# The state space gates as one product of 512 columns with the tokens at rest, in place of two of 256

## The chip, the core and the metric

The kernel runs on one core of a Trainium2 chip. Its time is device microseconds from the start to the end of one execution. Three runs of the kernel before gave a median of 1881.25 us (1880.52 to 1882.83). In the text PE is TensorE, DVE is VectorE, ACT is ScalarE, POOL is GpSimd and SP is the engine whose queue issues nearly all the DMAs.

## What is computed

A backbone of two layers over 256 latent and 256 context tokens of width 1024. Each layer is a half-step SwiGLU, a token mixer and a second half-step SwiGLU. The mixer projects the normalized tokens with `w_in`, splits the columns over three parallel groups (a gated linear recurrence of width 256, an attention of width 256, and a state space scan of width 512), and joins their outputs with `w_out`. In the last layer only the latent tokens go on behind the mixer. The change touches the columns z of `w_in`, 512 of them, which gate the state space part:

```
def mamba2_output(y, xs, z, d_skip, w):
    b, L = y.shape[:2]
    y = (y + d_skip[:, None] * xs).reshape(b, L, D_SSM)
    return rms_norm(y * jax.nn.silu(z), w)
...
    out_lat = jnp.concatenate([hg_lat, na_lat, ssm_lat], axis=-1) @ w_out
```

## The kernel before

All 512 tokens (context in columns 0 to 255, latent behind) stay on the core, features on the partitions, as eight tiles of 128 features. Every float32 product is made of three matmuls on rounded halves: a weight chunk `raw` of 128 x 1024 is loaded by SP, ACT casts it to `hi` (L291), DVE subtracts to get `lo` (L294), and `mm3` (L675 to L677) runs high by high, high by low and low by high. A chunk holds eight blocks of 128 columns in the order of `weight_plan`; `hi` and `lo` have two buffers each, `raw` three.

PSUM has eight banks, handed out by tags d, e, m and n with two each. A tile of a tag waits until the tile that held its buffer has been read. Tag n serves the attention's scores and transposes (`psm("n")`), tag d the projections.

Most projections keep a weight block at rest and stream 512 tokens. Some keep tokens at rest: 128 tokens of `hh` and `hl` are the stationary operand, and weight columns are streamed. The gates z are such a product. `tokens` makes 256 columns for each token tile and puts two token tiles into one bank, so that four token tiles take two banks of tag d (layer 0) and two take one (layer 1, where only the latent tiles 2 and 3 are needed). This is done twice, for the two halves of z; each half is evicted by ACT with Silu into `zs` (tag gm, L1400). Behind the state space scan `ssm` multiplies by `zs` (L1382), takes the mean square (L1383), normalizes, transposes (L1391) and splits into `mx` for `w_out`.

The order of the mixer is a list written by hand, `MIX_ORDER`: "feat", "feats", "feats1" and "tok" are dense projections, "go" starts a generator (`hg` for the recurrence, `na` for the attention, `ssm` for the scan) and "run" lets the started generators go on. The gates come last, behind all generators. The framework's scheduler then reorders the instructions of each engine within what the data and the buffers allow, so that dense matmuls come to stand between the steps of the generators. In a generator's step of attention, PE makes the scores of one head and one token tile (L1191) into a tile of tag n, DVE adds the bias (L1194, latent tiles only) and takes the maximum (L1196), ACT takes the exponential (L1198), PE transposes (L1203) into the other tile of tag n, ACT copies it (L1205), and PE multiplies by the values (L1207) into the scores' tile. Context tiles have 256 keys, latent tiles 512. After the last head the outputs are normalized (L1215, Newton steps from L557, L1218), transposed into two more tiles of tag n (L1223) and read by ACT and DVE (L873, L874). The recurrence `hg` has six levels of PE scores (L1069), DVE products (L1094) and an ACT copy (L1083), then transposes (L1105), state updates (L1116, L1127) and outputs (L1139, L1141, L1149, L1159). The scan has state updates (L1313, L1317, L1330), and for each token tile a product L1342, masks L1346, and weights L1366 to L1369 for the matmul L1374. `w_out` begins with the halves of the recurrence and the attention; its banks have the tags d, d, m, m, n, n in layer 0 and d, d, m, m in layer 1.

Of the kernel before, what the change touches and what calls it, by code (L numbers as in the profile page):

```python
# [12 lines left out]
AF = mybir.ActivationFunctionType  # L13
# [4 lines left out]
P = 128  # L18
KT = D // P
# [27 lines left out]
C_QA, C_KA, C_VA = 1280, 1536, 1792  # L47
C_Z, C_XBC, C_DT = 2048, 2560, 3584
# [44 lines left out]
def weight_plan(layer):  # L93

    plan, twice = [], []

    def align():
        plan.extend([None] * (-len(plan) % CB))

    def use_twice(blocks):  # L100
        align()
        n = len(plan) // CB
        plan.extend(blocks)
        align()
        twice.extend(range(n, len(plan) // CB))

    def ffn(w13, w2, passes, lat_only):
        for fs in FPARTS:
            rest = list(fs)
            if fs is FPARTS[0]:  # L110
                group, rest = rest[:2], rest[2:]
                blocks = [(w13, k, c, P) for k in range(KT) for f in group for c in (f * P, DFF + f * P)]
                plan.extend(blocks + blocks[:-2 * CB] * (passes - 1))
            for f in rest:
                for c in (f * P, DFF + f * P):
                    plan.extend((w13, k, c, P) for k in range(KT))
            tail = [] if lat_only or fs is not FPARTS[-1] else TAIL_F
            for d in range(KT):
                if d not in tail:
                    plan.extend((w2, f, d * P, P) for f in fs)  # L120
            if tail:
                use_twice([(w2, f, d * P, P) for d in tail for f in fs])
        align()

    def feat(c):
        plan.extend(("w_in", k, c, P) for k in range(KT))

    def tok(c):
        if c == C_VA:

            for k in range(0, KT, 3):
                align()
                plan.extend(("w_in", j, a, n) for j in range(k, min(k + 3, KT)) for a, n in ((c, 256), (C_DT, 16)))
                align()
            return
        for k in range(KT):
            plan.extend(("w_in", k, c + j, P) for j in (0, P))

    last = layer == DEPTH - 1
    ffn("ffn1_w13", "ffn1_w2", 1 if layer == 0 else 2, False)  # L140
    for step in MIX_ORDER[layer]:
        if step[0] in ("feats", "feats1"):
            blocks = [("w_in", k, c, P) for k in range(KT) for c in step[1:]]
            plan.extend(blocks + (blocks[:-2 * CB] if step[0] == "feats" else []))
        elif step[0] == "feat":
            feat(step[1])
        elif step[0] == "tok":
            tok(step[1])
    for ks in WOUT_K[layer]:
        for d in range(WOUT_N[layer]):  # L150
            plan.extend(("w_out", k, d * P, P) for k in ks)
    if not last:
        use_twice([("w_out", k, d * P, P) for d in TAIL_D for k in range(KT)])
    ffn("ffn2_w13", "ffn2_w2", 1 if last else 2, last)
    return plan, twice


def second(n):
# [17 lines left out]
        ("feat", C_C), ("run", 2), ("run", 4), ("feat", C_XS), ("feat", C_XS + 128), ("feat", C_XS + 256),  # L176
        ("feat", C_KA), ("dt",), ("go", "ssm"), ("run", 999), ("feat", C_QA), ("feat", C_KA + 128),
        ("go", "na"), ("run", 999), ("feats1", C_FF + 128, C_FB + 128, C_Q + 128, C_G + 128), ("go", "hg", 1),
        ("run", 999), ("tok", C_Z), ("tok", C_Z + 256), ("run", 999),
    ],  # L180
    [
        ("feats", C_FF, C_FB, C_Q, C_G), ("go", "hg", 0), ("tok", C_I), ("run", 999), ("tok", C_VA),
# [1 line left out]
        ("feat", C_B + 128), ("feat", C_C), ("feats1", C_FF + 128, C_FB + 128, C_Q + 128, C_G + 128),  # L184
        ("go", "hg", 1), ("run", 999), ("feat", C_XS), ("feat", C_XS + 128), ("feat", C_XS + 256),
        ("feat", C_XS + 384), ("dt",), ("go", "ssm"), ("run", 999), ("feat", C_KA + 128),
        ("feat", C_QA + 128), ("go", "na"), ("run", 999), ("tok", C_Z), ("tok", C_Z + 256), ("run", 999),
    ],
]

# [1 line left out]
def host_layout(inp):  # L192
# [39 lines left out]
    for l in range(DEPTH):  # L232
        plan = weight_plan(l)[0]
        for i in range(0, len(plan), CB):
            w, o = np.zeros((P, CB * P), np.float32), 0
            for name, k, c, n in filter(None, plan[i:i + CB]):
                w[:, o:o + n] = g[name][l][k * P:(k + 1) * P, c:c + n]
                o += n
            chunks.append(w)
# [15 lines left out]
class Weights:  # L255


    def __init__(self, b):
        self.b = b
        self.n = 0  # L260
        self.loads, self.raws = 0, []
        self.splits, self.parts = 0, []
        self.hold = 0
        self.at = 0
        self.after = ()
        self.twice = set()
        n = 0
        for l in range(DEPTH):
            plan, twice = weight_plan(l)
            self.twice.update(n + c for c in twice)  # L270
            n += len(plan) // CB
        self.chunks = n
# [73 lines left out]
class Build:  # L346
# [576 lines left out]
    def mixer(self, l, last):  # L923
        tc = self.tc
        self.l, self.last = l, last
        self.lo = CTX if last else 0
        self.tts = [2, 3] if last else [0, 1, 2, 3]
        self.mx = {}
        self.have = set()
        self.gs, self.qk, self.xf, self.bc = {}, {}, {}, {}  # L930
        self.active = {}
        with tc.tile_pool(name=self.nm("px"), bufs=1, reuse_waits="tile") as self.px:

            self.nc.sync.dma_start(out=self.xd, in_=self.x)
            self.xt4, self.ys4 = self.x[:, 0:4], self.x[:, 4:8]
            lat_only = (C_Q, C_G, C_QA, C_C)
            for step in MIX_ORDER[l]:
                if step[0] in ("feat", "feats", "feats1"):
                    cs = step[1:]
                    lo = [self.lo if any(b <= c < b + 256 for b in lat_only) else 0 for c in cs]  # L940
                    if len(cs) == 1:
                        pss = [self.feat([(lo[0], T)])]
                    elif step[0] == "feats1":
                        pss = self.group([(0, T)], "ddmm", lo)
                    else:
                        pss = self.group([(0, CTX), (CTX, T)], los=lo)
                    for c, lo, ps in zip(cs, lo, pss):
                        self.feature(c, lo, ps)
                elif step[0] == "tok":
                    c = step[1]  # L950
                    if c == C_VA:
                        self.va_in(self.tokens_dt())
                    else:
                        ps = self.tokens(self.tts if c >= C_Z else [0, 1, 2, 3])
                        if c >= C_Z:
                            self.z_in((c - C_Z) // 256, ps)
                        else:
                            self.v_in(ps)
                    self.have.add(c)
                elif step[0] == "go":  # L960
                    self.active[getattr(self, step[1])(*step[2:])] = None
                elif step[0] == "run":
                    self.pump(step[1])
                else:
                    getattr(self, step[0])()
            self.pump()
            assert not self.active
            if self.stop == "mix_%d" % l:
                self.dump_mix()
                return  # L970
            for k in range(0, KT, 2):
                self.nc.sync.dma_start(out=self.x[:, k:k + 2], in_=self.xd[:, k:k + 2])
            self.w_out(l, last)
            if last:
                self.raw_rstd()
                self.head = self.raw_group()
# [318 lines left out]
    def ssm(self):  # L1295
# [13 lines left out]
        for i in range(3):  # L1309
            for d in range(2):  # L1310
                t, t2 = order[d][i], order[d][i + 1]
# [3 lines left out]
                ps = self.psm("e")  # L1315
# [21 lines left out]
        for t in self.tts:  # L1337
            s = slice(t * P, (t + 1) * P)
# [9 lines left out]
            for g in range(2):  # L1348
                pa = self.psm("e")
                for d, m in ((0, self.slr), (1, self.sur)):  # L1350
                    for i, src in enumerate((self.ah, self.al)):
                        gm = self.tt("gm", [P, 4, P], F32R)
# [22 lines left out]
                                     start=True, stop=True)  # L1375
                nc.vector.tensor_tensor(out=y[:, gs], in0=y[:, gs], in1=py[:, :256], op=ALU.add)
                yield
        yield lambda: C_Z in self.have and C_Z + 256 in self.have
        nt = len(self.tts)
        ss = self.small([P, 4], "sss", 1)  # L1380
        for i, t in enumerate(self.tts):
# [11 lines left out]
            self.mx[4 + f] = self.split(mk, lo, T, pf[:, lo:], self.p(l, "ssn", f))  # L1393
            yield

    def z_in(self, j, ps):
        if j == 0:
            self.zs = {t: self.tt("gm", [P, 512]) for t in self.tts}
        for t in self.tts:
            self.nc.scalar.activation(self.zs[t][:, j * 256:j * 256 + 256], ps[t], AF.Silu)  # L1400

    def w_out(self, l, last):
        nc = self.nc
# [158 lines left out]
```

## Time and profile before

| | before |
|---|---|
| median of 3 runs | 1881.25 us (1880.52 to 1882.83) |
| the profiled execution, its own time | 1881.97 us |
| its span, first to last instruction | 1880.2 us |
| PE busy in the span | 1852.1 us, 99% |
| DVE busy | 1317.0 us, 70% |
| ACT busy | 724.8 us, 39% |
| POOL busy | 59.3 us, 3% |
| mean granted clock of PE, as a share of full speed | 0.995 |

The busy time of an engine is the time in which at least one of its instructions was running. The granted clock is the share of PE's full clock that the chip let through. All times of rows below are microseconds from the start of the span of this one execution, the durations of single instructions in the grouped list nanoseconds.

### The profile page before, as it was taken

Reading aid. Unit: us, or ns where it says so; the run is one execution under the profiler, and the core shown is the slowest. Engines: PE = TensorE matmul, PEld = TensorE weight load, DVE = VectorE, ACT = ScalarE, POOL = GpSimd, SP = SyncE. Lnnn points to the kernel's source line nnn. Section 1 sums busy time; section 2 is a strip of 40 time slices with the busy share of each in tenths; the row PEclk is TensorE's granted clock in tenths of the full one; section 3 lists DMA queues with packets and bytes.
Section 4 is the critical chain, followed back from the end, with each engine's and each line's share of the span. In section 5 each row is a group of like instructions: output and inputs, shape, how many; then the busy total and the mean of one; then the engine's idle time right before and its main releaser. Section 6 shows DMA issues by size and latency. Waiting matters only on the chain.

```text
span 1880.2 us, 28238 instructions
## 1 busy us (share of the span) xinstructions
PE 1852.1 (99%) x11235; PEld 1596.1 (85%) x11235; DVE 1317.0 (70%) x2324; ACT 724.8 (39%) x1160; POOL 59.3 (3%) x76
## 2 busy tenths in 40 slices
PE   9999999999999999999999999999999999999998
PEld 7788888899777889888888898888889987889998
DVE  7677877875877677677733557777637668887565
ACT  4332223334425544232223342222234455465454
POOL 1000000000014000000000000000000000210000
PEclk9999999999999999999999999999999999999999
DMA  8466666634212134566533536666434422245554
GB/s 307 156 193 194 197 190 194 185 138 124 79 40 62 47 116 143 163 195 192 163 94 101 158 112 189 193 194 194 126 101 154 144 91 74 91 142 183 181 180 134
DMA packets 76964, 277.83 MB, mean 148 GB/s; under 512 B 8608, under 2 KB 10016, under 8 KB 76320
## 3 DMA queue, kind: packets, MB, share of 16 engines
q1 hardware_dynamic: 75312, 272.88, 46.2%
q10 hardware_dynamic: 1520, 3.15, 0.5%
q8 instruction: 88, 1.44, 0.3%
q14 instruction: 44, 0.36, 0.1%
HBM read 269.71 MB, written 5.24 MB: 146 GB/s over the span
## 4 chain that ended last, share of the span: by engine, by line
PE 92%; DVE 6%; ACT 1%; issue 1%; DMA 0%; SPq 0%; DVEq 0%; ACTq 0%
PE psd L675 28%; PE psd L676 27%; PE psd L677 27%; PE psm L1069 1%; DVE junk L516 1%; PE psm L1191 1%; PE psm L1207 1%; PE psm L1317 1%; PE psm L1374 1%; DVE ew L1367 1%; PE psm L1330 1%; DVE lo L294 0%; PE psm L1358 0%; PE psm L592 0%; PE psm L578 0%
## 5 line engine op out<-in xcount | busy, mean ns | idle before, releaser
L294 DVE TENSOR_TENSOR lo<-raw,hi 128x1024 fp32r<-128x1024 f32 x328 | 403.7, 1231 | 369.0 <-ACT hi L291 365.4
L291 ACT CAST hi<-raw 128x1024 fp32r<-128x1024 f32 x332 | 348.6, 1050 | 715.8 <-PE psd L676 664.5
L675 PE MATMUL psd<-h,hi 128*128 128x512 f32 (+1 forms) x1456 | 539.0, 372 | 2.0 <-ACT h L655 1.0
L676 PE MATMUL psd<-h,hi 128*128 128x512 f32 (+1 forms) x1456 | 537.7, 370 | 0.5 <-DVE h L656 0.5
L677 PE MATMUL psd<-h,lo 128*128 128x512 f32 (+1 forms) x1456 | 536.5, 370 | 0.2 <-DVE lo L294 0.2
L516 DVE CUSTOM_DVE_ANT_0 junk<-wm,csb,par 128x1024 bf16<-128x1024 f32 x256 | 327.8, 1280 | 2.4
L675 PEld LDWEIGHTS psd<-h,hi 128*128 128x128 f32 x1456 | 273.5, 189 | 50.0 <-issue 1.5
L677 PEld LDWEIGHTS psd<-h,lo 128*128 128x128 f32 x1456 | 274.1, 188 | 48.4 <-issue 1.5
L676 PEld LDWEIGHTS psd<-h,hi 128*128 128x128 f32 x1456 | 274.6, 189 | 45.6 <-DVE h L656 0.9
L675 PE MATMUL psd<-gh,hi 128*128 128x512 f32 (+1 forms) x605 | 216.8, 358 | 0.0
L677 PE MATMUL psd<-gh,lo 128*128 128x512 f32 (+1 forms) x605 | 216.4, 358 | 0.0
L676 PE MATMUL psd<-gl,hi 128*128 128x512 f32 (+1 forms) x605 | 216.4, 358 | 0.0
L675 PEld LDWEIGHTS psd<-gh,hi 128*128 128x128 f32 x605 | 114.3, 189 | 17.0 <-ACT gh L813 0.3
L676 PEld LDWEIGHTS psd<-gl,hi 128*128 128x128 f32 x605 | 114.2, 189 | 16.7
L677 PEld LDWEIGHTS psd<-gh,lo 128*128 128x128 f32 x605 | 114.2, 189 | 16.7
L676 PE MATMUL psd<-raw,hi 128*128 128x258 f32 x352 | 99.7, 284 | 0.0
L675 PE MATMUL psd<-raw,hi 128*128 128x258 f32 x352 | 99.6, 284 | 0.0
L677 PE MATMUL psd<-raw,lo 128*128 128x258 f32 x352 | 99.3, 284 | 0.0
L813 ACT CAST gh<-silu 128x512 fp32r<-128x512 f32 (+1 forms) x88 | 49.7, 566 | 86.0 <-DVE silu L810 83.6
L544 DVE SCALAR_TENSOR_TENSOR x<-psd,gate,x 128x256 f32<-128x256 f32 x112 | 52.0, 480 | 36.6 <-PE psd L677 35.8
L675 PE MATMUL psd<-hi,h 128*128 128x256 f32 (+1 forms) x224 | 65.9, 295 | 1.4 <-ACT ga L1037 1.3
L675 PEld LDWEIGHTS psd<-raw,hi 128*128 128x128 f32 x352 | 67.0, 190 | 0.0
(276 smaller groups left out, 2435.5 us busy)
## 6 DMA issues: line engine op xcount, KB each, us to landing
raw<-in_wst SPq DMA_DIRECT2D x349, 512.0 KB, 3.6
wm<-in_wmod SPq DMA_DIRECT2D x128, 512.0 KB, 4.1
ws<-in_wm SPq DMA_DIRECT2D x8, 512.0 KB, 9.9
xd<-x SPq DMA_DIRECT2D x2, 2048.0 KB, 6.5
x<-xd SPq DMA_DIRECT2D x8, 512.0 KB, 4.1
wc<-in_wmod SPq DMA_DIRECT2D x7, 512.0 KB, 10.0
x<-in_xt SPq DMA_DIRECT2D x4, 512.0 KB, 5.3
n<-in_bias SPq DMA_DIRECT2D x8, 256.0 KB, 3.3
```

Source lines behind the costliest of these rows:

```text
L291: cut = nc.scalar.copy(hi, r)
L294: ins = e.tensor_tensor(out=lo, in0=r, in1=hi.bitcast(F32), op=ALU.subtract)
L516: self.nc.vector.tensor_tensor_reduce(junk, w, self.csb[:, v], 1.0, self.p(l, "bmod", j), ALU.mult, ALU.add, accum_out=self.mod[l][:, j, v ...
L544: ins = nc.vector.scalar_tensor_tensor(out=self.x[:, d, a:b], in0=ps[:, a - off:b - off], scalar=gate[:, d, v:v + 1], in1=self.x[:, d, a:b ...
L675: mm(ps, wh, xh, start=start, stop=False)
L676: mm(ps, wh, xl, start=False, stop=False)
L677: mm(ps, wl, xh, start=False, stop=stop)
L813: nc.scalar.copy(a[:, lo:hi], s[:, lo:hi])
L1069: nc.tensor.matmul(ps[r, s], kc[r, s], q(r, c * 64), start=True, stop=True)
L1191: nc.tensor.matmul(ps[:, :nk], self.qk[h2][r, t * P:(t + 1) * P], self.qk[2 + h2][r, :nk], start=True, stop=True)
L1207: nc.tensor.matmul(ps[:, hc], pT[:, k * P:(k + 1) * P], self.V[:, k, 256 + h * 64:256 + h * 64 + 64], start=k == 0, stop=k == nk // P - 1)
L1317: nc.tensor.matmul(ps[:, g * 256:g * 256 + 256], bt[:, t, g * P:(g + 1) * P], xw[:, g * 256:g * 256 + 256], start=True, stop=True)
```

## The change

The two products of 256 columns become one of 512: for each of the eight feature tiles k, four weight blocks (512 columns, half a chunk) are streamed against each token tile at rest. Each token tile has a bank of its own, of the tags d, d, n, n in layer 0 and d, d in layer 1. The matmuls are half as many and twice as wide (192 to 96 in layer 0, 96 to 48 in layer 1, the three of each `mm3` counted). The weights' order in the plan follows. Silu evicts 512 columns at a time.

```
         elif step[0] == "tok":
             tok(step[1])
+        elif step[0] == "gates":
+            plan.extend(("w_in", k, C_Z + j * P, P) for k in range(KT) for j in range(4))
...
-        ("run", 999), ("tok", C_Z), ("tok", C_Z + 256), ("run", 999),
+        ("run", 999), ("gates",), ("run", 999),
...
-        ("feat", C_QA + 128), ("go", "na"), ("run", 999), ("tok", C_Z), ("tok", C_Z + 256), ("run", 999),
+        ("feat", C_QA + 128), ("go", "na"), ("run", 999), ("gates",), ("run", 999),
...
-        yield lambda: C_Z in self.have and C_Z + 256 in self.have
+        yield lambda: C_Z in self.have
...
-    def z_in(self, j, ps):
-        if j == 0:
-            self.zs = {t: self.tt("gm", [P, 512]) for t in self.tts}
-        for t in self.tts:
-            self.nc.scalar.activation(self.zs[t][:, j * 256:j * 256 + 256], ps[t], AF.Silu)
+    def gates(self):
+
+        banks = [self.psd(tag) for tag in "ddnn"[:len(self.tts)]]
+        for k in range(KT):
+            wh, wl = self.w.next(4)
+            for t, q in zip(self.tts, banks):
+                s = slice(t * P, (t + 1) * P)
+                self.mm3(q, self.hh[k][:, s], self.hl[k][:, s], wh, wl, k == 0, k == KT - 1)
+        self.zs = {t: self.tt("gm", [P, 512]) for t in self.tts}
+        for t, q in zip(self.tts, banks):
+            self.nc.scalar.activation(self.zs[t], q, AF.Silu)
+        self.have.add(C_Z)
```

The scheduler decides where these matmuls stand on PE. In the rows below lines are those of the kernel that the rows come from; in the changed kernel the mixer's lines up to here are 2 lower (L1201 there is L1203 before) and those of `mm3` 2 higher (L677 is L675). `psm` are the small products' tiles of PSUM, `psd` those of the projections, `h` the normalized tokens, `con` holds the identity, `n` the attention's probabilities, `V` the values, `qk` queries and keys, `ga` the recurrence's factors.

Place 1 is PE in layer 0, in the attention's rounds over latent tokens. The kernel before has between the transposes of one head (L1203) and the values of that head (L1207) gate matmuls, into banks psd_5874 and psd_5875:

```order
L1203 MATMUL psm_5240<-con,n_897_5237 128x128 x4
L675 MATMUL psd_5874<-hi_5814,h_3213 128x256
L676 MATMUL psd_5874<-lo_5815,h_3213 128x256
L677 MATMUL psd_5874<-hi_5814,h_3214 128x256
L675 MATMUL psd_5874<-hi_5814,h_3213 128x256
L676 MATMUL psd_5874<-lo_5815,h_3213 128x256
L677 MATMUL psd_5874<-hi_5814,h_3214 128x256
L1207 MATMUL psm_5233<-V_3729,n_899_5245 128x64 x4
L1191 MATMUL psm_5252<-qk_4991,qk_3617 128x512
L1069 MATMUL psm_5596<-ga_5438,h_944_5594 64x64 x16
```

The changed kernel at the same heads:

```order
L1189 MATMUL psm_5233<-qk_4991,qk_3617 128x512
L1067 MATMUL psm_5573<-ga_5438,h_942_5571 64x64 x16
L1201 MATMUL psm_5240<-con,n_897_5237 128x128 x4
L1205 MATMUL psm_5233<-V_3729,n_899_5245 128x64 x4
L1189 MATMUL psm_5252<-qk_4991,qk_3617 128x512
L1067 MATMUL psm_5596<-ga_5438,h_944_5594 64x64 x16
L1201 MATMUL psm_5259<-con,n_901_5256 128x128 x4
```

The gate matmuls have gone from between the steps of both chains; 24 of them (banks psd_5756 and psd_5757, k of 0 to 3) stand ahead, the last beside the head in psm_5163.

Place 2 is PE in layer 0 behind the attention's last transposes. Before, the last gate matmuls, among them these, follow there, and then the recurrence's outputs (L1139):

```order
L1223 MATMUL psm_5305<-con,no_4997 128x128
L677 MATMUL psd_5875<-hi_5878,h_3218 128x256
L675 MATMUL psd_5875<-hi_5878,h_3217 128x256
L676 MATMUL psd_5875<-lo_5879,h_3217 128x256
L677 MATMUL psd_5875<-hi_5878,h_3218 128x256
L675 MATMUL psd_5874<-hi_5878,h_3219 128x256
```

After, the first matmuls into the banks of tag n (psd_5758, psd_5759) stand there, with the first weight chunk (hi_5410):

```order
L1221 MATMUL psm_5296<-con,no_4997 128x128
L1221 MATMUL psm_5305<-con,no_4997 128x128
L1114 MATMUL psm_5633<-V_3729,kS_5619 64x64
L677 MATMUL psd_5758<-hi_5410,h_3207 128x512
L678 MATMUL psd_5758<-lo_5411,h_3207 128x512
L679 MATMUL psd_5758<-hi_5410,h_3208 128x512
L677 MATMUL psd_5758<-hi_5410,h_3209 128x512
L677 MATMUL psd_5759<-hi_5410,h_3207 128x512
```

Of the gates' 192 narrow matmuls 24 stood behind L1223; of the 96 wide ones 72 stand there now, ahead of `w_out`. In layer 1 the 48 wide matmuls stand within the same rounds of attention and scan as the 96 narrow ones did.

## Rows read from the trace of the kernel before

**Rows 1.** The page's first part: busy time and share of each engine.

```profile
PE 1852.1 (99%) x11235; PEld 1596.1 (85%) x11235; DVE 1317.0 (70%) x2324; ACT 724.8 (39%) x1160; POOL 59.3 (3%) x76
```

**Rows 2.** PE's waits from 600 to 700: total us, times, longest.

```profile
PE psd L675 <- ACT ga L1037: 1.3, 1, 1.3
...
PE psm L1159 <- DVE h L1153: 0.2, 1, 0.2
```

**Rows 3.** Timeline of PE, attention rounds of layer 0: start, duration, instruction.

```profile
624.18 0.70 PE L1191 MATMUL psm<-qk,qk 64*128 64x256 f32 x2
...
628.09 0.70 PE L1191 MATMUL psm<-qk,qk 64*128 64x256 f32 x2
...
646.18 1.12 PE L1191 MATMUL psm<-qk,qk 64*128 64x512 f32 x2
...
649.96 0.60 PE L1203 MATMUL psm<-con,n 128*128 128x128 f32 x4
...
651.29 1.10 PE L1207 MATMUL psm<-V,n 128*128 128x64 f32 x8
652.33 1.12 PE L1191 MATMUL psm<-qk,qk 64*128 64x512 f32 x2
```

**Rows 4.** Grouped list, shapes apart: count, busy us, mean ns, idle before.

```profile
L676 PE MATMUL psd<-lo,h 128*128 128x256 f32 x160 | 46.5, 291 | 0.0
...
L675 PE MATMUL psd<-h,hi 128*128 128x512 f32 x1168 | 459.4, 393 | 1.0 <-DVE cv L1238 0.5 <-ACT silu L809 0.2 <-DVE dtk L1015 0.2
...
L294 DVE TENSOR_TENSOR lo<-raw,hi 128x1024 fp32r<-128x1024 f32 x328 | 403.7, 1231 | 369.0 <-ACT hi L291 365.4 <-PE psd L676 3.0
```

**Rows 5.** Timeline of PE, a run of 22 gate matmuls, first and last.

```profile
614.28 0.28 PE L675 MATMUL psd<-hi,h 128*128 128x256 f32 x1
...
616.78 0.28 PE L675 MATMUL psd<-hi,h 128*128 128x256 f32 x1
```

**Rows 6.** Timeline of PE, a run of 13 matmuls of 512 columns, first and last.

```profile
598.75 0.39 PE L676 MATMUL psd<-h,hi 128*128 128x512 f32 x1
...
601.50 0.39 PE L676 MATMUL psd<-h,hi 128*128 128x512 f32 x1
```

**Rows 7.** Timeline of all engines, the head whose scores start at 646.18.

```profile
647.40 0.43 DVE L1194 TENSOR_TENSOR psm<-psm,n 128x256 f32<-128x256 f32 x1 [0.83 <-PE psm L1191]
647.87 0.69 DVE L1196 TENSOR_REDUCE nsm<-psm 128x1 f32<-128x512 f32 x1
...
648.59 0.69 ACT L1198 ACTIVATE n<-psm,nsm 128x512 f32<-128x512 f32 x1 [2.98 <-DVE nsm L1196]
```

**Rows 8.** Timeline, layer 0, from the last head's values to w_out.

```profile
657.06 1.10 PE L1207 MATMUL psm<-V,n 128*128 128x64 f32 x8
...
661.98 1.17 PE L1223 MATMUL psm<-con,no 128*128 128x128 f32 x8
...
663.80 1.41 DVE L874 SCALAR_TENSOR_TENSOR qk<-psm,par,qk 128x512 fp32r<-128x512 f32 x2 [0.31 <-ACT qk L873]
...
666.89 0.30 PE L1139 MATMUL psm<-h,V 64*64 64x64 f32 x3 [0.40 <-DVE kS L1127]
...
669.74 0.50 PE L675 MATMUL psd<-mx,hi 128*128 128x512 f32 x1
```

**Rows 9.** Windows (length, busy, then PEclk, DMA, GB/s) and one wait, earlier in layer 0.

```profile
522.00:526.00 4.00, 1.98 (x15) 1.43 (x15) 3.29 (x5) 1.07 (x2) 2.67 (x3) 1.00 0.00 0
526.00:530.00 4.00, 3.82 (x57) 2.52 (x55) 0.81 (x2) 0.59 (x1) 0.00 (x0) 0.67 0.00 0
530.00:534.00 4.00, 4.00 (x23) 3.22 (x20) 3.07 (x13) 0.59 (x1) 0.00 (x0) 0.91 0.01 4
...
525.38 1.13 PE L1317 MATMUL psm<-s,bt 128*128 128x256 f32 x4 [2.02 <-DVE s L1313]
```

**Rows 10.** Windows of layer 1, before and after L1342 (PE, weight loads, DVE, ACT, POOL busy).

```profile
1600.00:1630.00 30.00, 29.64 (x179) 24.00 (x179) 23.23 (x43) 10.19 (x20) 0.91 (x1) 1.00 0.30 96
1630.00:1660.00 30.00, 25.93 (x180) 22.63 (x180) 27.23 (x72) 19.19 (x45) 9.96 (x12) 1.00 0.26 75
```

More of the change, by code (lines that the diff above doesn't have):

```diff
@@ L953, in mixer @@
                     else:
[L954 to L958, printed above, removed]
+                        self.v_in(self.tokens([0, 1, 2, 3]))
                     self.have.add(c)
```

## The prediction

> **What bounds the kernel now.** I read the profile from the whole to the stage. The engine table [rows 1] has TensorE (PE) busy 99% of the span and VectorE 70%, so a change counts by what it does to the order and the spacing of PE's instructions, and a faster ScalarE or VectorE is worth something only where PE waits for it. The list of PE's waits in the 100 us around the gates of layer 0 [rows 2] shows how little that is: its longest is 1.3 us, just before the first gate matmul, its shortest 0.2 us behind them. The timeline [rows 3] shows why. PE takes its instructions in order. The attention (L1191 scores, L1203 transposes, L1207 values) and the recurrence (L1069) are chains that go from PE to VectorE and ScalarE and back, and in their pauses stand gate matmuls.
>
> **The wide matmul itself.** By the grouped list [rows 4] a 256-column matmul lasts 291 ns and a 512-column one 393 ns, which looks like a third off for the same work. But matmuls are pipelined and these durations overlap; what PE pays is the distance between starts. In a run of gate matmuls [rows 5] 22 start from 614.28 to 616.78: 2.50 / 21 = 0.119 us each. In a run of 512 columns [rows 6] 13 start from 598.75 to 601.50: 2.75 / 12 = 0.229 us. Two halves cost 0.238, one whole 0.229: 0.009 us saved for each of the 96 pairs in layer 0 and the 48 in layer 1, 0.9 + 0.4 = 1.3 us in all. The Trainium skill, "Perfetto Trace Analysis", Matmuls, says that larger matmuls are more efficient than smaller ones; the rows agree with the direction and make the gain small.
>
> **Layer 0, where the order moves.** Before, the gates hold two PSUM banks at a time, both of tag d. Now all four token tiles stay open: two banks of tag d and two of tag n. Tag n is what the attention uses for scores and transposes, and its two buffers come round only when its last transposes have been read (L873, L874). The order shows what follows: only 24 of the 96 wide matmuls (banks d, first two weight chunks) stand within the rounds, the last beside the head in psm_5163. From there PE's row has nothing but L1203, L1207, L1191 and L1069 in turn, then L1105, L1116 and L1223, and the other 72 wide matmuls stand behind L1223. Both weight chunks in use are held until then, so banks d can't run ahead either.
>
> The walk starts where both kernels still agree, at the scores of psm_5163, 624.18 [rows 3]. The next two rounds have 256 keys; one took 3.91 us (to 628.09) with gate matmuls in it, and I take that for the bare round too, because the recurrence goes round with it. First scores of 512 keys: 632.0. A round of 512 keys took 6.15 us (646.18 to 652.33). In [rows 7] its reduction ended at 648.56 and the exponential ran to 649.28, but L1203 started at 649.96, 0.68 us late, because gate matmuls stood ahead of it. Bare it takes 6.15 - 0.68 = 5.47 us. Three of these lead to the last head's scores at 648.4, and its values are out 651.29 + 1.10 - 646.18 - 0.68 = 5.5 us later, at 653.9. In the trace of before they were out at 658.16 [rows 8]: the bare chain is some 4 us quicker, but no gate matmul is done meanwhile. From the values to L1223 it is 661.98 - 658.16 = 3.8 us (squares, Newton steps, scaling on the other engines), and from there until L874 has read the first bank 663.80 + 0.70 - 661.98 = 2.5 us: the n banks are free at 660.2. Then the 72 matmuls, 72 x 0.229 = 16.5 us, and between them the block L1139/L1141, which took 669.74 - 666.89 = 2.9 us. w_out begins at 679.6. (L1149 and L1159 stand ahead of w_out now and behind its start before; they are left out on both sides.) Before, w_out begins at 669.74 [rows 8]. Loss: **9.9 us**, with the 0.9 us of the wide matmul already in it.
>
> The shortest walk that I can defend: a 256-key round is half of a 512-key one, 2.7 us, and half of a round's six handovers vanish (0.10 us each, as from the end of L1191 at 647.30 to L1194 at 647.40 [rows 3, 7]). That is 2 x 1.2 + 4 x 0.3 = 3.6 us less, a loss of 6.3 us. Nothing behind the stretch gives it back: from 669.74 on PE waits 0.2 us in the list [rows 2], so there is no idle time that late work could fill.
>
> **The clock.** In every window of before that I read near the gates PE's granted clock is 1.00. But the trace has one place like the coming one [rows 9]: PE waited 2.02 us until 525.38, was busy 1.98 us of the 4 up to 526 and then ran short matmuls; the granted clock was 0.67 in the next 4 us and 0.91 in the 4 after. Of its two levels, 2.4 and 1.2 GHz, it was on the lower for (0.33 + 0.09) x 4 / 0.5 = 3.4 us, which loses 1.7 us of work. Between 653.9 and 660.2 PE will have L1116, L1223 and little else, some 3 us of work in 6.3, a share close to 1.98 of 4. I take one such fall there, **+1.7 us**; bounds 0 (the clock holds) and the second rival below. The Trainium skill, "TensorE: Matmul & The Clock Gate", HAM oscillation, warns of just this: pauses between bursts of matmuls send the clock back to half.
>
> **Layer 1.** Only token tiles 2 and 3, so two d banks as before and no n bank; 96 matmuls of 256 become 48 of 512, spread over the same rounds. Until L1342 PE works nearly all the time (29.64 of 30 us); after it VectorE leads, busy 27.23 of 30 us against PE's 25.93 [rows 10]. The order puts 40 wide matmuls (9.2 us) ahead of L1342 where 67 narrow ones (8.0) stood, which makes it 1.2 us later, and moves one weight subtraction of VectorE (L294, 1.23 us [rows 4]) from behind L1346 to a place ahead of it. These about cancel: **0**, bounds -0.4 (the dense saving alone) and +1.2.
>
> **At nothing.** The last two weight chunks can now be cast and subtracted only when the n-bank matmuls release a buffer. Twelve of these free the first buffer; three more, the 2.9 us of L1139/L1141 and ten more, 5.9 us in all, cover the 1.23 us of L294 and the cast ahead of it; uncovered, two chunks would cost twice the pair, some 4 us. Weight loads stay in order on their queue and wait for the same buffers, the two bias loads now behind one of them fewer; a chunk is used up every 24 matmuls, 5.5 us. On ScalarE the gate activations halve in number, and the first two run beside PE's last n-bank matmuls, so the d banks are free when w_out wants them.
>
> **Sum.** 9.9 + 1.7 + 0 = 11.6 us. The profiled execution took 1881.97, which is 0.72 above the median 1881.25; held against the median, 1892.9 us.
>
> **Rivals.** *Wide is cheap:* PE pays the durations of the grouped list. Then layer 0 saves 192 x 0.291 - 96 x 0.393 = 18.1 us and layer 1 half of that, 27 in all, against 11.6: 1865.7 us, faster. It decides from 11.6 / 144 = 0.08 us a pair on; the starts [rows 5, 6] give 0.009. Chance 5%. The Trainium skill, "TensorE: Matmul & The Clock Gate", Back-to-back issue gap, points the same way with a sustained 131 ns for 512 columns; the starts 229 ns apart contradict it here. *The clock falls in the rounds too:* PE's own share of a 512-key round is 1.12 + 0.60 + 1.10 = 2.8 us [rows 3], which the lower level could double at most; part of it is not columns, so 1.5 to 2.8 us a round. Four such rounds, the two smaller and the recurrence's end give 6 to 11 us more: 1899 to 1904. Against it: layer 1 held 1.00 with PE waiting 4 us in 30 [rows 10], and no pause within a round is as long as the 2.02 us of [rows 9]. 15%. *Short rounds:* the shortest walk with the clock held, 6.3: 1887.6 us, 12%. *No change:* the pauses are shorter still, and less than 3.8 us is lost; nearly every piece would have to lie below its row. 6%. The forecast, 1889 to 1897, has 62%.
>
> **Numbers.** Faster 0.05; within 0.2% (3.8 us, about what a measurement of this kernel can tell from no change) 0.06; slower 0.62 + 0.15 + 0.12 = 0.89. The range 1886 to 1901 takes in the forecast, most of the short rounds and a third of the clock rival.
>
> **What would show it.** Right: waits of PE of some 10 us in all before L1203, L1207, L1191 and L1069 between 625 and 655, where there are none now; rounds of 512 keys of about 5.5 us; a gap before L1223; the n-bank gates from near 660 and w_out from near 680; wide gates 0.229 us apart; a clock below 1.00 around 655 to 664; layer 1 within 1 us. Wrong: gate matmuls less than 0.2 us apart, rounds below 5 us, or the clock at its lower level from 630 on.

## The result, and the profile after

The changed kernel took 1904.16 us (median of 4, 1901.46 to 1905.89) against 1882.04 for the kernel before in the same comparison: ratio 1.0114, 95% interval 1.0101 to 1.0126 (ratios here are taken over all executions, and so differ a little from those of the medians). Forecast were 1892.9 us and a range of 1886 to 1901. The direction held; the loss is 22 us and not 11. The profiled execution took 1902.71 us, its span is 1901.0, 20.8 longer than before.

The page's first and second part: busy time by engine, and PE's granted clock in 40 slices of 47.5 us.

```profile
PE 1863.6 (98%) x11091; PEld 1597.1 (84%) x11091; DVE 1315.5 (69%) x2324; ACT 722.4 (38%) x1152; POOL 58.0 (3%) x76
...
PEclk8999999999999799999999999999999999999999
```

Against [rows 1] PE has 144 matmuls fewer and is busy 11.5 us longer, and the 14th digit, 618 to 665 us, is a 7. (The 8 at the start is a stretch far ahead of the gates; the runs of each layer, below, come back to it.) Windows of that stretch (length, busy PE, PEld, DVE, ACT, POOL with counts, then the clock):

```profile
628.00:632.00 4.00, 2.97 (x42) 2.19 (x42) 2.57 (x7) 1.85 (x5) 0.00 (x0) 1.00 0.20 66
632.00:636.00 4.00, 2.82 (x39) 1.79 (x40) 3.24 (x8) 1.40 (x3) 0.00 (x0) 1.00 0.02 4
636.00:640.00 4.00, 3.27 (x30) 2.21 (x32) 2.31 (x7) 1.20 (x2) 0.00 (x0) 0.96 0.09 28
640.00:644.00 4.00, 2.78 (x29) 2.19 (x25) 2.88 (x6) 1.88 (x4) 0.00 (x0) 0.50 0.14 37
...
656.00:660.00 4.00, 3.71 (x37) 3.12 (x33) 2.96 (x7) 1.99 (x7) 0.00 (x0) 0.50 0.00 0
...
664.00:668.00 4.00, 3.41 (x50) 2.87 (x44) 2.35 (x12) 0.86 (x2) 0.00 (x0) 0.63 0.00 0
668.00:672.00 4.00, 3.07 (x14) 2.55 (x14) 3.55 (x14) 0.44 (x2) 0.00 (x0) 1.00 0.02 4
```

PE waits in every window until 640, at the full clock; from there to 664 the granted clock is 0.50, the lower of its two levels (1.2 GHz). It is back at 1.00 by 667, by the 0.63 of the window from 664 to 668, and so before the first dense gate matmul at 668.93. PE's waits from 624 to 656, where the kernel before has none, and its timeline there, which answers to [rows 3, 8] (the scores L1191, transposes L1203 and values L1207 of before are L1189, L1201 and L1205 here):

```profile
PE psm L1205 <- ACT n L1203: 3.0, 5, 0.7
PE psm L1201 <- ACT n L1196: 1.5, 4, 0.6
PE psm L1067 <- ACT h L1081: 0.6, 1, 0.6
```

```profile
625.04 0.70 PE L1189 MATMUL psm<-qk,qk 64*128 64x256 f32 x2
...
632.46 1.12 PE L1189 MATMUL psm<-qk,qk 64*128 64x512 f32 x2
634.15 1.15 PE L1067 MATMUL psm<-ga,h 64*64 64x64 f32 x32 [0.57 <-ACT h L1081]
635.90 0.66 PE L1201 MATMUL psm<-con,n 128*128 128x128 f32 x4 [0.60 <-ACT n L1196]
637.29 1.10 PE L1205 MATMUL psm<-V,n 128*128 128x64 f32 x8 [0.73 <-ACT n L1203]
638.32 1.12 PE L1189 MATMUL psm<-qk,qk 64*128 64x512 f32 x2
...
645.38 2.07 PE L1189 MATMUL psm<-qk,qk 64*128 64x512 f32 x2
...
653.32 2.07 PE L1189 MATMUL psm<-qk,qk 64*128 64x512 f32 x2
...
668.93 0.47 PE L677 MATMUL psd<-hi,h 128*128 128x512 f32 x1 [1.46 <-DVE qk L876]
...
690.29 0.50 PE L677 MATMUL psd<-mx,hi 128*128 128x512 f32 x1
```

A round of 512 keys takes 5.86 us at the full clock (632.46 to 638.32) and 7.94 at the lower (645.38 to 653.32); scores grow from 1.12 to 2.07 us. The first gate matmul in a bank of tag n starts at 668.93 (forecast 660.2) and `w_out` at 690.29 (679.6; before 669.74 [rows 8]).

The wide gate matmuls themselves are as forecast: 12 of them start from 677.81 to 680.31, 2.50 / 11 = 0.227 us apart.

### The profile page after: what moved, and what is told of

The parts are those of the page before. It is cut to its first block, busy times and chain, and to the rows that moved or that the text cites. A ratio compares the mean times of both kernels' runs of the same rounds, so it can differ in the third digit from the quotient of the medians.

```text
span 1901.0 us, 27945 instructions
## 1 busy us (share of the span) xinstructions
PE 1863.6 (98%) x11091; PEld 1597.1 (84%) x11091; DVE 1315.5 (69%) x2324; ACT 722.4 (38%) x1152; POOL 58.0 (3%) x76
## 4 chain that ended last, share of the span: by engine, by line
PE 91%; DVE 5%; ACT 2%; issue 1%; DMA 1%; DVEq 0%; SPq 0%; ACTq 0%
PE psd L677 27%; PE psd L678 27%; PE psd L679 27%; PE psm L1189 1%; PE psm L1205 1%; PE psm L1067 1%; PE psm L513 1%; DVE ew L1365 1%; PE psm L1315 1%; PE psm L1372 1%; PE psm L1201 0%; DVE lo L296 0%; ACT hi L293 0%; PE psm L1328 0%; PE psm L594 0%
## 5 line engine op out<-in xcount | busy, mean ns | idle before, releaser
L677 PE MATMUL psd<-h,hi 128*128 128x512 f32 (+1 forms) x1456 | 538.7, 372 | 2.0 <-ACT h L657 1.0
L677 PEld LDWEIGHTS psd<-h,hi 128*128 128x128 f32 x1456 | 273.4, 188 | 49.9 <-issue 1.5
L677 PE MATMUL psd<-gh,hi 128*128 128x512 f32 (+1 forms) x605 | 216.8, 358 | 0.0
L677 PEld LDWEIGHTS psd<-gh,hi 128*128 128x128 f32 x605 | 114.3, 189 | 17.0 <-ACT gh L815 0.3
L677 PE MATMUL psd<-raw,hi 128*128 128x258 f32 x352 | 99.6, 284 | 0.0
L678 PEld LDWEIGHTS psd<-raw,hi 128*128 128x128 f32 x352 | 67.0, 190 | 0.0
L677 PEld LDWEIGHTS psd<-raw,hi 128*128 128x128 f32 x352 | 67.0, 190 | 0.0
```

The source lines that it names most:

```text
L677: mm(ps, wh, xh, start=start, stop=False)
L678: mm(ps, wh, xl, start=False, stop=False)
```

## The experiments

Theories: *placement* (the gates wait for banks that the attention holds, so its rounds run bare, which costs their pauses), with the *clock* falling because of the bare rounds; rivals: *width* (512-column gate matmuls cost something themselves), and a clock that falls for another reason. Times stand beside the kernel before on the same chip.

**Banks of tag e.** Edit:

```
-        banks = [self.psd(tag) for tag in "ddnn"[:len(self.tts)]]
+        banks = [self.psd(tag) for tag in "ddee"[:len(self.tts)]]
```

> The changed kernel with one edit: the two extra banks of layer 0's gates come from tag e, which the state space scan has left by then, and not from tag n. Placement theory (the loss is there because the gates wait for the attention's banks; 512 columns cost nothing by themselves): gate matmuls stand in the attention's rounds again, the granted clock is 1.00 from 625 to 670, w_out starts at 669 to 672, and the whole saves at most the dense 1.3 us: 1880 to 1883 us. Width theory (512-column gate matmuls with tokens at rest cost more than the two halves, or lengthen the chains that they stand in): 1890 us or more.

1888.88 us against 1881.99, ratio 1.0029 (1.0015 to 1.0043). The rounds are filled again: PE busy 4.00 of 4 us in every window from 624 to 652, clock 1.00. So wide matmuls stand in the rounds without harm to them, which speaks against width; the next run settles it. But the gates, now used up early, leave the recurrence's end bare:

```profile
PE psm L1157 <- DVE h L1151: 3.0, 1, 3.0
```

Behind that wait, from 672 to 680, the clock is 0.85 and 0.73, and it is at 0.74 again from 1640 to 1660. The time lies between the two forecasts: the change of tag fills the rounds and opens another hole behind them.

**Wide in two passes, tag d alone** (layer 0's weights for the gates are then loaded twice).

```
+        for i in range(0, len(self.tts), 2):
+            pair = self.tts[i:i + 2]
+            banks = [self.psd() for _ in pair]
...
-        for k in range(KT):
+            for k in range(KT):
```

> Wide gate matmuls in two passes in layer 0: token tiles 0 and 1 into two banks of tag d, then tiles 2 and 3 into two of tag d, the weights loaded, cast and subtracted a second time (four chunks more: 2 MB, 4 x 1.05 us of ACT, 4 x 1.23 us of DVE, none of it on PE). No bank of tag n. Placement theory: the same dense cover as before, clock 1.00, w_out at 669 to 673, 1880 to 1885 us. Width theory: 1890 us or more.

1882.38 against 1881.99, ratio 1.0006 (0.9995 to 1.0016), clock 1.00 throughout the rounds. Wide matmuls cost nothing where the banks come free; four more chunks on DVE and ACT cost nothing either.

**The same banks, 256 columns.**

```
-                self.mm3(q, self.hh[k][:, s], self.hl[k][:, s], wh, wl, k == 0, k == KT - 1)
+                for o in (0, 256):
+                    self.mm3(q[:, o:o + 256], self.hh[k][:, s], self.hl[k][:, s], wh[:, o:o + 256], wl[:, o:o + 256],
+                             k == 0 and o == 0, k == KT - 1 and o == 256)
```

> The changed kernel with each 512-column gate matmul cut back to two of 256, in both layers, everything else left: four open banks of tags d, d, n, n in layer 0. Placement theory: the rounds are bare as in the changed kernel, the clock falls to its lower level near 640, and the time is that of the changed kernel or up to 1.3 us more: 1903 to 1907 us. Width theory: near the kernel before, 1881 to 1884 us.

1898.7 us against 1881.99, ratio 1.0091 (1.0072 to 1.011), below the expected 1903 to 1907. Most of the loss is there with no wide matmul in the kernel, and so is the clock's fall, from 0.58 in 636 to 640 to 0.73 in 672 to 676 (the traced execution, 1903.36, was the longest of the four). With the run before, placement is shown from both sides: wide matmuls without the loss, and the loss without wide matmuls.

**Banks of tag m**, which the recurrence holds ("ddmm" in the same line).

> The changed kernel with layer 0's two extra banks of tag m, which the recurrence holds, in place of tag n, which the attention holds. Placement theory, in its general form (the gates start when the chain that holds the tag has let go of it): the rounds are as bare as in the changed kernel, the clock is at the lower level from about 640, and the 72 gate matmuls now stand behind the recurrence's last matmuls and not between them; the recurrence's chain to there is bare too: w_out at 692 to 697, 1901 to 1909 us. If only the attention's tag matters: 1881 to 1885 us.

1914.51 against 1883.68, ratio 1.0167 (1.0147 to 1.0187): the same bare rounds, and then the recurrence's end bare too. PE's longest waits from 640 to 690:

```profile
PE psm L1137 <- DVE kS L1125: 4.0, 1, 4.0
PE psm L1157 <- DVE h L1151: 3.0, 1, 3.0
```

It is above the expected 1901 to 1909: I had not counted these two waits, in which no gate matmul can stand any more, and the clock is at its lower level again for some 7 us behind each.

**Idle matmuls in the bare rounds.** Three, then two, at each of ten places in the last five rounds (`pp` is the transposes' tile, `ps` the scores'):

```
+                    fill = nt == 4 and h2 == 1 and (t >= 2 or t == 1 and h == 3)
+                    for _ in range(2 if fill else 0):
+                        nc.tensor.matmul(pp, self.hh[0][:, :P], self.hh[1], start=True, stop=True)
...
+                    for _ in range(2 if fill else 0):
+                        nc.tensor.matmul(ps, self.hh[0][:, :P], self.hh[1], start=True, stop=True)
```

> The changed kernel with idle matmuls added in the last five bare rounds of layer 0: in each, three of 512 columns ahead of the transposes and three ahead of the values, written to a PSUM tile that the kernel overwrites or does not read, so that the result stays the same. They add 30 x 0.229 = 6.9 us of PE's work, about as long as the waits that they stand in. Clock theory (the bare rounds cost 9.9 us, and a further 8 to 10 us come from the clock, which falls because PE is half idle in them): granted clock 1.00 to about 655, rounds of 512 keys 5.3 to 6.0 us, w_out at 680 to 683, 1892 to 1896 us. If the clock falls for another reason: the lower level from 640 on as in the changed kernel, 1904 us or more.

1902.34 against 1881.99, ratio 1.0105 (1.0086 to 1.0124). Not clean: three at each place changed the order, with a new wait of 2.3 us for the first 512-key exponentials; the clock was 0.69 from 632 to 636 and 0.50 from 636 to 644, but 1.00 from 648 to 660, inside the filled rounds. The time is nearer to the forecast for a fall with another reason, so this run alone speaks for neither.

> As the run with idle matmuls in the bare rounds, but two in place of three at each of the ten places, so that PE's order stays that of the changed kernel (one recurrence matmul apart), and no new wait comes from the filling. 20 x 0.229 = 4.6 us of added work, in waits of 0.5 to 0.7 us each. Clock theory: the granted clock is 1.00 through the rounds to about 656, rounds of 512 keys take 5.4 to 5.9 us as at full clock, w_out starts 8 us sooner than in the changed kernel, at 680 to 684, and the time is 1893 to 1897 us: what is left is the cost of bare rounds. If the clock falls for another reason: 1902 us or more, lower level from 640 on.

1894.02 against 1881.9, ratio 1.0075 (1.0062 to 1.0088). Windows, timeline and waits (624 to 656) of PE in that run:

```profile
632.00:636.00 4.00, 3.13 (x41) 1.94 (x40) 3.37 (x8) 1.40 (x3) 0.00 (x0) 1.00 0.00 0
636.00:640.00 4.00, 3.74 (x31) 2.11 (x31) 2.56 (x6) 1.21 (x2) 0.00 (x0) 1.00 0.15 53
640.00:644.00 4.00, 3.29 (x39) 2.46 (x34) 2.65 (x7) 1.98 (x4) 0.00 (x0) 1.00 0.04 12
...
656.00:660.00 4.00, 2.77 (x63) 2.28 (x64) 3.06 (x16) 0.98 (x3) 0.00 (x0) 1.00 0.02 4
```

```profile
623.65 0.70 PE L1189 MATMUL psm<-qk,qk 64*128 64x256 f32 x2
...
631.57 1.12 PE L1189 MATMUL psm<-qk,qk 64*128 64x512 f32 x2
...
637.79 1.12 PE L1189 MATMUL psm<-qk,qk 64*128 64x512 f32 x2
...
643.53 1.12 PE L1189 MATMUL psm<-qk,qk 64*128 64x512 f32 x2
...
649.19 1.12 PE L1189 MATMUL psm<-qk,qk 64*128 64x512 f32 x2
...
661.68 0.47 PE L677 MATMUL psd<-hi,h 128*128 128x512 f32 x1 [1.46 <-DVE qk L876]
```

```profile
PE psm L1204 <- ACT n L1196: 1.6, 4, 0.5
PE psm L1210 <- ACT n L1206: 1.0, 4, 0.3
```

The clock is 1.00 all the way through the rounds, and adding 4.6 us of work that nothing reads took 10 us off the changed kernel. The filling is not free: behind most of the idle matmuls PE still waits for the same releasers, but in the last round of 256 keys no wait is left. From the scores that both kernels still reach alike to the second scores of 512 keys this run takes 637.79 - 623.65 = 14.14 us, the changed kernel 638.32 - 625.04 = 13.28, both at the full clock. The rest, 12 us above the kernel before, is the bare rounds and up to 0.9 us of this.

> As the run with two idle matmuls at each of ten places, but only those five ahead of the values: 10 x 0.229 = 2.3 us of added work, and the waits for the exponentials (0.5 to 0.6 us each) stay empty. If any shortening of the pauses keeps the clock: 1893 to 1897 us, clock 1.00 in the rounds. If what was left of the pauses is enough for it to fall: between, or 1898 to 1902 us with the lower level from somewhere behind 640 on.

1896.72 against 1883.68, ratio 1.008 (1.0054 to 1.0106). Windows, waits (624 to 656) and timeline of PE in the profiled execution, 1893.73 us:

```profile
632.00:636.00 4.00, 2.82 (x40) 1.74 (x39) 3.56 (x9) 1.46 (x4) 0.00 (x0) 1.00 0.02 4
...
640.00:644.00 4.00, 2.81 (x16) 1.95 (x16) 2.38 (x7) 1.88 (x4) 0.00 (x0) 1.00 0.02 7
644.00:648.00 4.00, 2.71 (x41) 1.72 (x39) 3.18 (x7) 1.44 (x4) 0.00 (x0) 1.00 0.02 4
```

```profile
PE psm L1202 <- ACT n L1196: 4.1, 5, 1.1
PE psm L1208 <- ACT n L1204: 1.1, 4, 0.3
PE psm L1067 <- ACT h L1081: 0.6, 1, 0.6
```

```profile
624.33 0.70 PE L1189 MATMUL psm<-qk,qk 64*128 64x256 f32 x2
...
637.62 1.12 PE L1189 MATMUL psm<-qk,qk 64*128 64x512 f32 x2
...
661.50 0.47 PE L677 MATMUL psd<-hi,h 128*128 128x512 f32 x1 [1.46 <-DVE qk L876]
...
682.88 0.51 PE L677 MATMUL psd<-mx,hi 128*128 128x512 f32 x1
```

The clock held at 1.00 with PE in these windows no busier than in the changed kernel before its fall, and with ten waits of 5.8 us in all, the longest 1.1, where the changed kernel has ten of 5.1, the longest 0.73. Up to the second scores of 512 keys it runs like the changed kernel (13.29 us against 13.28), so this filling delays nothing there. Two of the four executions took 1899.72 and 1901.13 us. They have no trace, but the mean granted clock is on record for each: 0.991 in these two, 0.994 and 0.995 in the others. So half the filling holds the clock in some executions and not in all.

**Layer by layer.** Layer 1's change alone, then layer 0's alone (the other layer's lines as before):

```
-        ("feat", C_QA + 128), ("go", "na"), ("run", 999), ("tok", C_Z), ("tok", C_Z + 256), ("run", 999),
+        ("feat", C_QA + 128), ("go", "na"), ("run", 999), ("gates",), ("run", 999),
```

> The kernel before with the change in layer 1 alone (layer 0 keeps its two products of 256 columns). By the prediction's step on layer 1: 0, between -0.4 and +1.2 us, so 1881 to 1884 us and a clock of 1.00 in layer 1's rounds. By what the changed kernel's trace showed: PE's waits before the values matmul of the scan (for the weights of DVE) go from 2.1 to 3.6 us, the longest from 0.8 to 1.9, worth +0.8 us while the clock holds; where such a wait sets the clock back, as in the run with tag e (980.9 us from layer 0's to layer 1's residuals against 974.8), some 6 us: median 1882 to 1888 us.

1881.51 against 1881.9, ratio 1.0005 (0.9995 to 1.0015): nothing, as predicted.

> The kernel before with the change in layer 0 alone, banks of tags d, d, n, n (layer 1 keeps its two products of 256 columns). If the loss is layer 0's: 1899 to 1904 us, the lower clock level from about 640 to 665. If layer 1 carries a part of it: as many us less than the changed kernel's 1904.

1897.87, ratio 1.0096 (1.0081 to 1.011), the lower level from 640 to 665 as in the changed kernel. The loss is layer 0's, except some 6 us. So the changed kernel ran again, unedited, twice with timing:

> The changed kernel again, beside the two below on one chip. The parts so far: layer 0 alone gave 1897.9, layer 1 alone no difference; their sum is 1897 to 1900, and the changed kernel's first timing 1904.2. If nothing but the parts is in it: 1897 to 1902 us here. If the two layers' changes cost more together than apart: 1903 to 1906 us again.

1905.42 against 1883.68, ratio 1.0118 (1.0098 to 1.0137).

> The changed kernel once more, beside layer 0's part alone on one chip. If layer 1's wide product costs something in most executions: 4 to 7 us above layer 0's part alone, and this trace or the next shows the lower clock level between 1640 and 1680. If it was scatter between chips: within 2 us of layer 0's part alone.

> Layer 0's part alone once more. If layer 1's wide product costs something in most executions: 1897 to 1900 us, with the clock at 1.00 in layer 1. If it was scatter between chips: within 2 us of the changed kernel.

1903.0 and 1896.45 on one chip, ratios 1.0116 (1.0101 to 1.0132) and 1.008 (1.0068 to 1.0093). The 6 us are no scatter between chips. But the profiled executions of the changed kernel in these two runs took 1897.75 and 1896.71 us, with no fall of the clock in layer 1: here the executions that are longer are those without a trace. A further trace of each kernel, with

> A further trace of the changed kernel: where the clock is below 1.00, and how long layer 0 and layer 1 take in this execution. Lower level from about 640 to 665 in any case; in an execution of 1903 us or more, by the layer 1 reading, also 3 to 10 us between 1640 and 1700.

> A further trace of layer 0's part alone: lower level from about 640 to 665; by the layer 1 reading no fall, or a shorter one, between 1640 and 1700.

gave 1899.54 and 1898.21 us and the same picture: lower level from the 630s to about 664 and 658, 1.00 in layer 1.

The mean granted clock, on record for every execution, says more. In the second comparison on one chip the three untraced executions of the changed kernel have 0.985 to 0.987 and its traced one 0.990; all five of layer 0's part alone have 0.990. With a lower level of 0.50, a mean of 0.985 means (1 - 0.985) x 1902 / 0.5 = 57 us there, 0.987 means 49 and 0.990 means 38. So the longer executions do spend some 11 to 19 us more at the lower level, which can cost up to half of that, 6 to 10 us. Where it lies is not shown for them. The one longer execution that has a trace is the first, 1902.71 us, and its extra stretch lies far ahead of the gates: the granted clock from 12 to 34 us, in that trace and in the one of 1897.75 us:

```profile
12.00:34.00 22.00, 21.04 (x98) 18.23 (x99) 13.53 (x33) 6.22 (x13) 2.34 (x1) 0.61 1.02 417
12.00:34.00 22.00, 21.90 (x130) 19.09 (x131) 14.97 (x33) 8.57 (x17) 5.20 (x2) 0.84 1.03 416
```

By the scores at 625.04 and 621.63 the first trace is 3.4 us behind ahead of the bare rounds. The last run filled the scan's waits in layer 1 (`py` is the values' tile):

```
+                for _ in range({(2, 0): 6, (3, 0): 3, (3, 1): 2}.get((t, g), 0) if self.last else 0):
+                    nc.tensor.matmul(py, self.hh[0][:, :P], self.hh[1], start=True, stop=True)
```

> The changed kernel with eleven idle matmuls of 512 columns (2.5 us) in layer 1's scan, six, three and two ahead of the three values matmuls that wait for DVE's weights there (1.95, 0.98 and 0.67 us in the changed kernel), written to columns that nothing reads or that are overwritten. Layer 0 is as changed. If a fall of the clock behind these waits is the extra 6 us of the timed executions: 1896 to 1900 us in all of them. If the 6 us are elsewhere: 1903 to 1906 us as in the changed kernel.

1904.46 against 1884.19, ratio 1.0111 (1.0094 to 1.0129), but it settles nothing: the order moved with it, and its trace has a wait of 5.1 us before L1221 in layer 1 and a clock of 0.84 and 0.82 behind it. Where in the kernel the 6 us are lost stays open.

**A better version?** Layer 0 with the banks e, e, d, d and layer 1 as before:

> Layer 0's 512-column gates in banks of tags e, e, d, d, layer 1 as in the kernel before. Against the first run with tag e it takes layer 1's wide product out, and w_out's matmuls stand between the recurrence's last two steps, where that run had a wait of 3.0 us and a fall of the clock. Placement theory: rounds filled, clock 1.00, at most 0.9 us gained from the wider matmuls: 1880 to 1883 us. If the wait of 3.0 us stays: 1883 to 1886 us. Width theory: 1888 us or more.

1883.97 against 1881.9, ratio 1.0007 (0.9995 to 1.0019): rounds filled, but a wait of 2.4 us before the recurrence's last transposes, and behind it a clock of 0.71 and 0.86 from 672 to 680. The traced execution, 1887.28 us, also has the clock at 0.50 from 1640 to 1650, in layer 1 as it was before. No version beat the kernel before. A reading that fits both runs with tag e: the dense gates are a fixed amount of cover, and what is used early is missing at the recurrence's end.

## Why the prediction was wrong

By the starts of `w_out`, each against the scores of the same head (624.18 before, 625.04 in the changed kernel, 624.33 with half the filling, whose traced execution kept the full clock):

- Changed kernel: 690.29 - 669.74 - 0.86 = 19.7 us later; seven more traces with the same layer 0 give 19.7 to 20.4. Half filled: 682.88 - 669.74 - 0.15 = 13.0.
- In both, 21.4 us pass from the first gate in an n bank to `w_out`, where I had 19.4. Of the 2.0 between, L1147 and L1157 are 1.4, which I left out since before they stand behind the start of `w_out`. Behind that start 1.5 us come back: up to the next SwiGLU's first matmul it is 48.1 us (738.40 - 690.29) in place of 49.6 (719.36 - 669.74). Its lines, before and after:

```profile
719.36 0.28 PE L675 MATMUL psd<-h,hi 128*128 128x256 f32 x1
738.40 0.28 PE L677 MATMUL psd<-h,hi 128*128 128x256 f32 x1
```

- That leaves 13.0 - 1.5 = **11.5 us for the bare rounds** (predicted 9.9) and 19.7 - 13.0 = **6.7 us for the clock** (predicted 1.7).

Of the 10.5 us by which the forecast's loss of 11.6 was short of the median's 22.1, that is 1.6 and 5.0. The 3.9 left stand in no trace; the 6 us of the longer executions, below, are the nearest to them. (The pieces come from single executions, which differ by up to 5 us ahead of the gates: the same scores start at 620.3 to 625.0 in the changed kernel's four traces. That is why I measure from a common instruction. Between medians layer 0's part alone costs 14 to 16 us, which would still lie in the range of 1886 to 1901; the 6 us, again time at the lower clock level, carry it out.)

**Layer 0's order: right.** The 72 matmuls stand where the order shows them, PE waits within the rounds, `w_out` follows them. (In the trace of the kernel before 28 and not 24 narrow ones stand behind L1223; the sum doesn't use them.) The term was 1.6 us short. From the common scores to the first gate in an n bank the half-filled run takes 661.50 - 624.33 = 37.2 us against 36.0: its rounds of 512 keys take 5.87, 5.73 and 5.66 us and not 5.47, and in the first the recurrence's turn waits too (0.6 us for L1081). The rest is what doesn't come back behind `w_out`.

**The clock: the step that failed.** I took "one such fall" behind the rounds, 3.4 us at the lower level for 1.7 us, bounded the other case as a rival at 15%, and argued against it that "no pause within a round is as long as the 2.02 us of [rows 9]". The clock fell inside the rounds, at 640, early in the third bare one; from 624 six waits of 2.9 us in all stood ahead of the fall, the longest 0.73 us. It stayed low to 667: 27 us, for 6.7. So the length of the longest pause was the wrong measure. Their sum is no better one: the half-filled run waited more in all and longer at a time, and held 1.00. What the runs show is that the bare rounds bring the fall, in all ten traces that have them (eight with the changed layer 0, and those with tag m and with 256 columns), and that two idle matmuls a place prevent it; what in the pauses decides stays open. The precedent doesn't carry either: the changed kernel's trace has the same wait of 2.0 us there, and no fall:

```profile
523.00:527.00 4.00, 2.91 (x21) 1.96 (x19) 3.93 (x5) 2.15 (x4) 4.00 (x4) 1.00 0.32 112
527.00:531.00 4.00, 2.86 (x38) 1.96 (x42) 0.97 (x3) 0.59 (x1) 0.26 (x1) 1.00 0.00 0
```

The Trainium skill, "TensorE: Matmul & The Clock Gate", A second HAM failure mode: psum-queue depth-cycling, tells of a kernel that cycles through PSUM banks and idles briefly between matmul groups so often that the clock swings. This trace agrees that short waits can be enough (0.73 us at most), but shows one fall and one rise and no swing. I had weighed the section before it, on long waits.

The 27 us cost 6.7 and not half of them. A round grew from 5.9 us (5.7 in the half-filled run) to 7.9 and not to double; that its steps on DVE and ACT keep their length is the likely reason, not tested by itself. The rival's 1899 to 1904 us came close to the time, but in part by luck: of its 6 to 11 us above the forecast, the clock in this stretch gave 5.0.

**Layer 1: right** alone, 1.0005. In the changed kernel's trace the scan's values wait a little longer than before (the first line is the kernel before, 1560 to 1700), and one wait ahead of layer 1's mixer is not there before:

```profile
PE psm L1374 <- DVE ew L1369: 2.1, 3, 0.8
PE psm L1372 <- DVE ew L1367: 3.6, 3, 1.9
...
PE psd L677 <- DVE x L546: 1.0, 1, 1.0
```

Of the 20.8 us between the spans, 0.9 were there before the gates and 18.2 (19.7 - 1.5) are layer 0's. Another 1.2 pass between layer 0's mixer and layer 1's attention, where that wait stands; two of the changed kernel's four traces have it, so it is not bound to the change. That leaves 0.4 for all behind it, the longer scan waits included.

**The wide matmul: right.** Starts 0.227 us apart, and 0.120 for the halves in the narrow run.

**Open:** the 6 us by which most of the changed kernel's executions exceed its three shorter traced ones and layer 0's part alone. That they go with more time at the lower clock level is shown by the mean granted clock; where it is spent in the untraced executions, and why it takes the changes of both layers together, is not.

## What to carry to other kernels

Before widening a product's output, ask who holds the PSUM buffers that it would open: here dense matmuls filled the chains' pauses only when their banks didn't come from a tag that one of the chains still held, and a product issued last on such a tag waited for that chain's end. The Trainium skill, "Perfetto Trace Analysis", Matmul Optimizations, advises having all eight banks in use; here two more open banks gained nothing: of tag n they cost 18 us in layer 0, of tag m 31 us in all, of tag e 2 us (7 with layer 1's change). When cover is taken from a stretch, don't conclude from the lack of one long pause that the clock will hold: price a fall over the whole stretch as a case of its own. Idle matmuls written where nothing reads them tell afterwards, in one run, what the clock cost.

## What the runs showed of the hardware

- The granted clock fell with no wait over 0.73 us, PE busy 2.8 to 3.3 of each 4 us at the full level; ten places with two idle matmuls each kept it at 1.00. With five such places it stayed at 1.00 in the traced execution, PE busy as little as 2.71 of 4 us and waiting up to 1.1 us at a time.
- The same code falls in one execution and not in the next: the wait near 525 us had a clock of 0.67 in [rows 9] and 1.00 in the changed kernel; layer 1's rounds held 1.00 in [rows 10] and were at 0.50 from 1640 to 1650 in one run with layer 1 unchanged.
- At the lower level 512-column matmuls start 0.43 us apart (682.45 to 682.88 in the run with tag m).
